# Reordered input projections, a smaller block solve, earlier feed-forward sums and a new load order in a hybrid decoder layer

## The chip, the cores and the metric

The kernel runs on one core of one Trainium2 chip. The metric is the device time of one execution in microseconds, on the core's own clock; the profile is of one execution of the same program.

## What is computed

One decoder layer on an input of 1024 tokens by 1024 features, float32. The reference, cut to what matters:

```python
h = rmsnorm(x, norm_mix)
proj = h @ w_in                                    # 1024 x 3360
q_nsa, kv_nsa, gate_nsa, qkv_gdn, z_gdn, b_gdn, a_gdn = split(proj)
o_nsa = rmsnorm(nsa_mixer(q_nsa, kv_nsa, gate_nsa, ...), nsa_norm)    # 8 heads of 64
o_gdn = gdn_mixer(qkv_gdn, z_gdn, b_gdn, a_gdn, ...)                  # 4 heads of 128
x = x + concat(o_nsa, o_gdn) @ w_out
u = causal_dwconv(rmsnorm(x, norm_ffn) @ ffn_up, ffn_conv)            # 2 x 2816 wide
gate, up = split(u)
x = x + (silu(gate) * up) @ ffn_down
return rmsnorm(x, norm_final)
```

nsa_mixer is sparse attention (compressed, selected and window branches). gdn_mixer is a gated delta rule: a causal convolution of width 4 on q, k and v, then for each chunk of 64 tokens a unit lower triangular system, solved by blocks of 32, and a state that is carried from chunk to chunk.

## The kernel before, in words

Tokens are worked on in 8 tiles of 128, or in two halves of 512. Large products run as float32r matmuls of 128 x 128 by 128 x 512. An operand is split into a high half (a cast to float32r on ScalarE, ACT) and a low half (the difference, on GpSimd, POOL, or on VectorE, DVE), and a product is the sum of high-high, high-low and low-high (`mm3`, from L122 to L128; the up product has the same in L1116, the down product in L1314). The program is given in the order of its functions; a planner with a model of the machine puts each engine's instructions in order, and `high_priority` and `issue_after` bias it. An engine then works through its own queue in order. All transfers are issued by SyncE (SP) from one queue.

**Input stage** (`phase_in`, L509). Activations are normalised and transposed into hH and hL. `proj_block` (L191) makes one block of 128 features by 512 tokens with 24 matmuls into one of two PSUM banks. `conv_block` (L448) loads and splits a tile of w_gdn (`split_weight`, L109; the POOL difference is L118), calls `proj_block`, copies the result twice to SBUF on ACT (L458, L463), applies three taps on DVE (L465), an activation (L468, L469), and stores to d_kqv. There are 12 tiles (0 to 3 make q, 4 to 7 k and 8 to 11 v), run for the first half of the tokens and then all for the second, each with its own load and split. The recurrence runs beside this with a higher priority: for a pair of tiles `gdn_pre` makes the blocks, `gdn_blocks` (L337) inverts 32 x 32 triangular blocks by 31 steps of two DVE instructions (L348, L350), with 32 columns spread over four partition groups and 8 columns a, and sends the result through DRAM (d_z) to `gdn_solve` (L355); `gdn_scan` carries the state. Further projections (z, q, compressed keys) fill the gaps.

**Attention** (`phase_attend`) holds the pools of its tiles, and pool og with the operand of the output product (mg). `phase_out` (L1006) does the output product of the last four tiles with operands mh and ml in a pool of its own (L1023, L1026), adds the residual, normalises (`norm_transpose`, L138) and puts high and low parts D (`put_parts`, L185).

**Feed-forward.** The up and down products use seven products instead of eight on 2 x 2 blocks, after two ordinary pairs of row tiles (`plain`) in the up product. The right-hand operands are sums of the four blocks B11, B12, B21 and B22 of the normalised input: T[0] to T[2], split in high and low parts. `norm_second` (L1049) makes them: s1 = B22 - B12 (L1088) as the transposes arrive, and the rest in `late` (L1092): 16 additions and subtractions with the split parts of D (`add`, L1073 to L1076) and three sets of four splits (L1070, L1071). `prepare` (L1183) makes the weight operands (L1140, L1142, L1153) of the next row tile, `convolve` and `put_away` do the convolution, the gate and the sums for the down product. `phase_down` (L1269) loads operands a_raw one pair at a time (L1301) and after each two entries of a queue of loads (L1294): weight quarters b11, b21, then the residual xr in eight row tiles, then b12 and b22. xr lies in the memory that the up product's row tiles held.

Of the kernel before, what the change touches and what calls it, by code (L numbers as in the profile page):

```python
# [46 lines left out]
def shape_constants():  # L47
# [11 lines left out]
    rho = i % 4  # L59
    for a in range(8):  # L60
        c[i, C_ZI + a * 32 + 8 * rho + a] = 1.0
# [129 lines left out]
def proj_block(K, w, b):  # L191

    wh, wl = w
    ps = K.pp.tile([P, 512], F32, name="proj_ps", tag="proj")
    d = slice(b * 512, (b + 1) * 512)
    mm3(K.nc, ps, [(wh[:, k * P:(k + 1) * P], wl[:, k * P:(k + 1) * P], K.hH[:, k, d], K.hL[:, k, d])
                   for k in range(NK)])
    return ps
# [138 lines left out]
def gdn_blocks(K, p):  # L337

    nc = K.nc
    db, dz = K.d_blk[p % 2], K.d_z[p % 2]  # L340
    bb = K.gt.tile([P, 32, 32], F32, name="bb", tag="bb")
    nc.sync.dma_start(bb, bc(db.rearrange("t b h j i -> (t b h) j i"), 1, 4))
    z = K.gt.tile([P, 8, 32], F32, name="zb", tag="zb")
    nc.vector.tensor_copy(z, K.zinit)
    for j in range(31):
        na, n = min(8, j + 1), 31 - j
        tmp = K.gt.tile([P, 8, 32], F32, name="ztmp", tag="ztmp", bufs=1)
        nc.vector.tensor_tensor(out=tmp[:, 0:na, 0:n], in0=bc(z[:, 0:na, j], 2, n), in1=bc(bb[:, j, j + 1:32], 1, na),  # L348
                                op=ALU.mult)
        nc.vector.tensor_tensor(out=z[:, 0:na, j + 1:32], in0=z[:, 0:na, j + 1:32], in1=tmp[:, 0:na, 0:n],  # L350
                                op=ALU.add)
    nc.sync.dma_start(dz.rearrange("t b h (r a) i -> (t b h r) (a i)", a=8), z.rearrange("p a i -> p (a i)"))


def gdn_solve(K, t, st):  # L355
# [3 lines left out]
    dz = K.d_z[t // 2 % 2][t % 2]  # L359
# [3 lines left out]
    for b in range(4):  # L363
        d = slice(32 * b, 32 * b + 32)
        nc.sync.dma_start(Z[d, :, d], dz[b].rearrange("h r i -> r h i"))
# [82 lines left out]
def conv_block(K, ct, b):  # L448
# [3 lines left out]
    ps = proj_block(K, split_weight(K, K.A["w_gdn"][ct]), b)  # L452
# [56 lines left out]
def phase_in(K, ctx):  # L509
# [45 lines left out]
    with ExitStack() as st:  # L555
# [17 lines left out]
        for ct in range(12):  # L573
            conv_block(K, ct, 0)
        for ct in range(12):
            conv_block(K, ct, 1)
# [386 lines left out]
def phase_attend(K, ctx):  # L963
    nc, tc = K.nc, K.tc
    mk = lambda n, b, **kw: ctx.enter_context(tc.tile_pool(name=n, bufs=b, **kw))
    for n in ("apl", "an", "aps", "asm", "ap", "og"):
        setattr(K, n, mk(n, 2 if n == "asm" else 1, side="right"))
# [38 lines left out]
def phase_out(K):  # L1006

    nc, tc, A = K.nc, K.tc, K.A
    with ExitStack() as st:
        xp = st.enter_context(tc.tile_pool(name="xo", bufs=2, side="right"))  # L1010
        po = st.enter_context(tc.tile_pool(name="po4", bufs=4, space=PSUM))
        px = st.enter_context(tc.tile_pool(name="pn2", bufs=4, space=PSUM))
        ws = K.ws
        for b, tiles in HALVES:
            for i in tiles:
# [5 lines left out]
                mh = xp.tile([P, 4, P], F32R, name="mh", tag="mh")  # L1021
                ml = xp.tile([P, 4, P], F32R, name="ml", tag="ml")
# [13 lines left out]
            if b:  # L1036
                norm_transpose(K, tiles, lambda j: K.x1[j],
                               lambda k, ps: put_parts(K, *K.D[k // 4][k % 4], ps,
                                                       K.vec[:, V_NFFN + k:V_NFFN + k + 1]), K.fw, px, "px", 4,
                               lambda j: row_tile(K, 4 + j))  # L1040


def row_tile(K, j):

    n = ("ga", "f_g", "f_u", "ga", "f_g", "f_u", "ga", "acc")[j]
    return K.fw.tile([P, 2 + SEQ], F32, name=n, tag=n, bufs={"ga": 3, "acc": 1}.get(n, 2))[:, 2:]


def norm_second(K):  # L1049
# [6 lines left out]
    K.T = [None] * 4  # L1056

    for j in (1, 2, 0, 3):
        h3 = K.late_pools.enter_context(tc.tile_pool(name=f"h3{j}", bufs=1))
        K.T[j] = [tuple(h3.tile([P, 512], F32R, name=f"t{n}{j}{k}") for n in "hl") for k in range(4)]  # L1060
# [12 lines left out]
    def add(out, x, j, k, op0, op1):  # L1073

        nc.vector.tensor_tensor(out=out, in0=x, in1=K.D[j][k][0].bitcast(F32), op=op0)
        nc.vector.tensor_tensor(out=out, in0=out, in1=K.D[j][k][1].bitcast(F32), op=op1)  # L1076

    def put(k, ps):
        g = K.vec[:, V_NFFN + k:V_NFFN + k + 1]
        if k < 4:  # L1080
            put_parts(K, *K.T[3][k], ps, g)
            b12[k] = scr("b12", 4)
            nc.scalar.activation(b12[k], ps, AF.Copy, scale=g)
            return
        k -= 4
        put_parts(K, *K.D[2][k], ps, g)
        s2 = s1[k] = scr("s1", 4)
        nc.vector.scalar_tensor_tensor(out=s2, in0=ps, scalar=g, in1=b12[k], op0=ALU.mult, op1=ALU.subtract)  # L1088
# [3 lines left out]
    def late():  # L1092
        for k in range(4):
            split(2, k, s1[k])
            add(b12[k], b12[k], 0, k, ALU.subtract, ALU.subtract)
            split(0, k, b12[k])
            add(s1[k], s1[k], 0, k, ALU.add, ALU.add)
            split(1, k, s1[k])
# [170 lines left out]
def phase_down(K, ctx, out):  # L1269
# [136 lines left out]
def open_common(K, ctx):  # L1406
# [36 lines left out]
    K.d_z = [dp.tile([2, 4, 4, 32, 32], F32, name=f"d_z{i}") for i in range(2)]  # L1443
# [3 lines left out]
def tile_hymba(ctx: ExitStack, tc: tile.TileContext, A, out):  # L1447
    K = Ctx()
    K.nc, K.tc, K.A = tc.nc, tc, A
    with ExitStack() as mix:  # L1450
        with ExitStack() as K.lctx:
# [6 lines left out]
            K.wn = mix.enter_context(tc.tile_pool(name="wn", bufs=2, side="right"))  # L1458
            with ExitStack() as st:
# [6 lines left out]
                for k in range(4)] for j in range(3)]  # L1466
        phase_out(K)
# [65 lines left out]
```

## Time and profile before

| | us |
|---|---|
| median of the runs (3) | 1486.92 |
| lowest and highest run | 1484.9, 1490.7 |
| the profiled execution | 1485.12 |
| its span, first to last instruction | 1483.3 |
| TensorE (PE) busy | 1423.7 (96%) |
| DVE, ACT, POOL busy | 1090.7, 688.1, 557.5 |

Times in the rows count from the start of the span. A group of instructions shows its line, engine, operation, out<-in, the shape and the count, then busy time, the mean of one in ns, and the idle time before it with what ended it. The matmuls of a group overlap: a mean of 400 ns in a dense stretch goes with one start every 0.23 us. The granted clock is the share of TensorE's full speed.

### The profile page before, as it was taken

To read this page: it belongs to the slowest core of one execution; us is meant where nothing else is said; L and a number is where in the kernel's file an instruction comes from. 1 tells how busy PE (TensorE), PEld (TensorE's weight loads), DVE (VectorE), ACT (ScalarE), POOL (GpSimd) and SP (SyncE) were. 2 spreads that over 40 slices of the span, in tenths; PEclk is the share of its full clock that TensorE was granted. 3 is DMA by queue.
4 is the path that set the end of the run, shared out by engine and by line. 5 is a ranking of instruction groups with operands and counts; after the bars stand their busy time and mean duration, and the time that the engine had idled before them with its cause. 6 is when DMAs were issued, how large, how long until landed. Compare 5 with 4: busy or idle time off the path is not lost.

```text
span 1483.3 us, 21381 instructions
## 1 busy us (share of the span) xinstructions
PE 1423.7 (96%) x7572; PEld 1144.8 (77%) x7572; DVE 1090.7 (74%) x2098; ACT 688.1 (46%) x1347; POOL 557.5 (38%) x547
## 2 busy tenths in 40 slices
PE   8998899999999999999999969999999999899997
PEld 8876677788877777777778848888888888778886
DVE  5768997887335686777546898888888887697656
ACT  7443343233233555678646444444444444333343
POOL 3356433344342343555555531111111112354444
PEclk9999999999999999999999989999999999999999
DMA  6245352344277544311225032322233326773334
GB/s 236 87 154 183 110 163 76 116 116 151 77 240 202 169 132 120 104 52 36 65 93 199 1 113 100 107 100 98 88 106 107 107 79 236 265 243 89 96 107 149
DMA packets 105627, 188.06 MB, mean 127 GB/s; under 512 B 17168, under 2 KB 52016, under 8 KB 105392
## 3 DMA queue, kind: packets, MB, share of 16 engines
q1 hardware_dynamic: 105520, 186.69, 38.9%
q8 instruction: 60, 0.98, 0.3%
q14 instruction: 47, 0.39, 0.1%
HBM read 135.00 MB, written 51.66 MB: 126 GB/s over the span
## 4 chain that ended last, share of the span: by engine, by line
PE 67%; DVE 16%; DMA 6%; issue 4%; ACT 4%; POOL 2%; SPq 0%; DVEq 0%; ACTq 0%; POOLq 0%
PE up_ps L1116 27%; PE dn_ps L1314 10%; PE po L890 4%; PE pt L877 4%; DVE cv_acc L465 3%; PE proj_ps L128 2%; PE proj_ps L126 2%; PE proj_ps L127 2%; PE s_ps L809 2%; PE s_ps L811 2%; DVE zb L350 1%; DVE ztmp L348 1%; PE og_ps L126 1%; PE og_ps L127 1%; PE og_ps L128 1%
## 5 line engine op out<-in xcount | busy, mean ns | idle before, releaser
L1314 PE MATMUL dn_ps<-d_op 128*128 128x512 f32 x924 | 213.9, 393 | 4.5 <-ACT d_op L1305 1.9
L1314 PEld LDWEIGHTS dn_ps<-d_op 128*128 128x128 f32 x924 | 174.8, 190 | 43.1 <-DVE d_op L1308 2.6
L128 PE MATMUL proj_ps<-hH,w_l 128*128 128x512 f32 x384 | 157.2, 409 | 6.9 <-POOL w_l L118 6.9
L126 PE MATMUL proj_ps<-hH,w_h 128*128 128x512 f32 x384 | 155.5, 407 | 3.6 <-ACT cv_acc L463 3.3
L127 PE MATMUL proj_ps<-hL,w_h 128*128 128x512 f32 x384 | 154.9, 403 | 0.0
L1306 POOL TENSOR_TENSOR d_op<-a_raw,d_op 128x1024 fp32r<-128x1024 f32 (+1 forms) x42 | 105.1, 2504 | 124.0 <-ACT d_op L1305 104.8
L1116 PE MATMUL up_ps<-th,op_h 128*128 128x512 f32 x336 | 133.3, 398 | 11.8 <-ACT op_h L1140 11.8
L1116 PE MATMUL up_ps<-tl,op_h 128*128 128x512 f32 x336 | 133.3, 397 | 0.0
L1116 PE MATMUL up_ps<-th,op_l 128*128 128x512 f32 x336 | 132.7, 396 | 0.0
L118 POOL TENSOR_TENSOR w_l<-w_raw,w_h 128x1024 fp32r<-128x1024 f32 (+2 forms) x46 | 109.5, 2386 | 53.5 <-ACT w_h L116 51.9
L1308 DVE TENSOR_TENSOR d_op<-b,d_op 128x1024 fp32r<-128x1024 f32 (+1 forms) x42 | 81.9, 1954 | 49.2 <-ACT d_op L1307 43.3
L1116 PE MATMUL up_ps<-dh,op_h 128*128 128x512 f32 x288 | 113.0, 398 | 1.4 <-ACT op_h L1140 1.4
L1116 PE MATMUL up_ps<-dl,op_h 128*128 128x512 f32 x288 | 113.7, 396 | 0.0
L1116 PE MATMUL up_ps<-dh,op_l 128*128 128x512 f32 x288 | 110.4, 395 | 0.0
L1228 DVE SCALAR_TENSOR_TENSOR ga<-f_g,vec,ga 128x1024 f32<-128x1024 f32 x44 | 91.0, 2068 | 11.1 <-ACT ga L1226 10.4
L1161 POOL MEMSET f_u<- 128x2 f32 x22 | 2.2, 100 | 253.0 <-DVE acc L1228 160.3
L128 PEld LDWEIGHTS proj_ps<-hH,w_l 128*128 128x128 f32 x384 | 74.1, 193 | 27.0 <-POOL w_l L118 10.9
L1140 ACT ACTIVATE op_h<-w_raw 128x1024 fp32r<-128x1024 f32 (+1 forms) x64 | 58.8, 923 | 71.8 <-PE up_ps L1116 69.9
L465 DVE SCALAR_TENSOR_TENSOR cv_acc<-cv_raw,vec,cv_acc 128x512 f32<-128x512 f32 x72 | 76.6, 1063 | 18.4 <-ACT cv_acc L463 17.6
L126 PEld LDWEIGHTS proj_ps<-hH,w_h 128*128 128x128 f32 x384 | 74.0, 193 | 19.4 <-ACT cv_acc L463 4.7
L1305 ACT ACTIVATE d_op<-a_raw 128x1024 fp32r<-128x1024 f32 (+1 forms) x42 | 41.3, 985 | 101.7 <-PE dn_ps L1314 47.8
L127 PEld LDWEIGHTS proj_ps<-hL,w_h 128*128 128x128 f32 x384 | 74.2, 193 | 15.6 <-DVE hL L188 0.4
(334 smaller groups left out, 3474.2 us busy)
## 6 DMA issues: line engine op xcount, KB each, us to landing
w_raw<-in_w_up_dram SPq DMA_DIRECT2D x44, 512.0 KB, 3.3
a_raw<-d_a SPq DMA_DIRECT2D x35, 512.0 KB, 3.6
w_raw<-in_w_gdn_dram SPq DMA_DIRECT2D x24, 512.0 KB, 3.7
d_a<-ga SPq DMA_DIRECT2D x44, 256.0 KB, 2.0
b<-in_w_down_dram SPq DMA_DIRECT2D x20, 512.0 KB, 6.6
d_a<-so SPq DMA_DIRECT2D x33, 256.0 KB, 2.0
qT<-d_q SPq DMA_DIRECT2D x32, 256.0 KB, 5.6
mg<-d_mix SPq DMA_DIRECT2D x16, 512.0 KB, 3.9
```

Source lines behind the costliest of these rows:

```text
L118: (low or nc.gpsimd).tensor_tensor(out=wl, in0=raw, in1=wh.bitcast(F32), op=ALU.subtract)
L126: nc.tensor.matmul(out, ah, bh, start=(i == 0), stop=False)
L127: nc.tensor.matmul(out, ah, bl, start=False, stop=False)
L128: nc.tensor.matmul(out, al, bh, start=False, stop=(i == n - 1))
L465: nc.vector.scalar_tensor_tensor(out=acc, in0=raw[:, j:j + 512], scalar=tap(j), in1=acc, op0=ALU.mult, op1=ALU.add)
L877: nc.tensor.transpose(pt[0:kk, h, :], src[h], K.ident)
L890: last = nc.tensor.matmul(po[64 * par:64 * par + 64], v, pT[:, par::2], start=(last is None or first), stop=(left == 0))
L1116: mm = lambda a, b, start, stop: nc.tensor.matmul(out, a, b, start=start, stop=stop, skip_group_check=not first)
L1228: nc.vector.scalar_tensor_tensor(out=a, in0=raw[:, j:j + SEQ], scalar=tap(j), in1=a, op0=ALU.mult, op1=ALU.add)
L1306: nc.gpsimd.tensor_tensor(out=al, in0=raw, in1=ah.bitcast(F32), op=ALU.subtract)
L1308: nc.vector.tensor_tensor(out=bl, in0=b[js.start], in1=bh.bitcast(F32), op=ALU.subtract)
L1314: one = lambda a, b, start, stop: nc.tensor.matmul(ps, a, b, start=start, stop=stop, skip_group_check=not first)
```

## The change

It has these parts. The title that it came with names grouped value products too; no line of the diff touches the value products of the attention.

- `proj_block`: the products with the low half of the weight come last.
- `phase_in`, `conv_block`: tiles 0 to 7 for the first half, then 8 to 11 for both halves with one load and split, then 0 to 7 for the second half.
- `gdn_blocks`, `gdn_solve`: column 4a + r in partition group r, so that step j needs j // 4 + 1 columns; d_z is laid out by row; bb is loaded in four pieces.
- `phase_attend`, `phase_out`: pool og outlives the attention and holds mh and ml; the PSUM pools of `phase_out` wait tile by tile.
- `phase_out`, `norm_second`: a copy b11 of block B11; t0 = B12 - B11, s1 = B22 - B12 and b12 = B22 - t0 are formed from PSUM; `late` only splits.
- `phase_down`: the residual is loaded in eight pieces of two row tiles by 512 columns, two of them after b11 and six at the end of the queue.

```diff
-    rho = i % 4
+    rho = i // 32
     for a in range(8):
-        c[i, C_ZI + a * 32 + 8 * rho + a] = 1.0
+        c[i, C_ZI + a * 32 + 4 * a + rho] = 1.0
...
-    mm3(K.nc, ps, [(wh[:, k * P:(k + 1) * P], wl[:, k * P:(k + 1) * P], K.hH[:, k, d], K.hL[:, k, d])
-                   for k in range(NK)])
+    jobs = [(wh, h, k) for k in range(NK) for h in (K.hH, K.hL)] + [(wl, K.hH, k) for k in range(NK)]
+    for n, (w, h, k) in enumerate(jobs):
+        K.nc.tensor.matmul(ps, w[:, k * P:(k + 1) * P], h[:, k, d], start=(n == 0), stop=(n == len(jobs) - 1))
...
-    nc.sync.dma_start(bb, bc(db.rearrange("t b h j i -> (t b h) j i"), 1, 4))
+    for r in range(4):
+        nc.sync.dma_start(bb[32 * r:32 * r + 32], db.rearrange("t b h j i -> (t b h) j i"))
...
-        na, n = min(8, j + 1), 31 - j
+        na, n = j // 4 + 1, 31 - j
...
-    nc.sync.dma_start(dz.rearrange("t b h (r a) i -> (t b h r) (a i)", a=8), z.rearrange("p a i -> p (a i)"))
+    nc.sync.dma_start(dz.rearrange("(a r) t b h i -> (r t b h) a i", r=4), z)
...
-        nc.sync.dma_start(Z[d, :, d], dz[b].rearrange("h r i -> r h i"))
+        nc.sync.dma_start(Z[d, :, d], dz[:, b])
...
-        for ct in range(12):
-            conv_block(K, ct, 0)
-        for ct in range(12):
-            conv_block(K, ct, 1)
+        for cts, bs in ((range(8), (0,)), (range(8, 12), (0, 1)), (range(8), (1,))):
+            for ct in cts:
+                w = split_weight(K, A["w_gdn"][ct], low=None)
+                for b in bs:
+                    conv_block(K, ct, b, w)
...
-        po = st.enter_context(tc.tile_pool(name="po4", bufs=4, space=PSUM))
-        px = st.enter_context(tc.tile_pool(name="pn2", bufs=4, space=PSUM))
+        po = st.enter_context(tc.tile_pool(name="po4", bufs=4, space=PSUM, reuse_waits="tile"))
+        px = st.enter_context(tc.tile_pool(name="pn2", bufs=4, space=PSUM, reuse_waits="tile"))
...
-                mh = xp.tile([P, 4, P], F32R, name="mh", tag="mh")
-                ml = xp.tile([P, 4, P], F32R, name="ml", tag="ml")
+                mg = K.og.tile([P, 4, 2 * P], F32R, name="mg", tag="mg", bufs=2)
+                mh, ml = mg[:, :, 0:P], mg[:, :, P:2 * P]
...
+                    put_parts(K, *K.D[k // 4][k % 4], ps, g)
+                    if k < 4:
+                        nc.scalar.activation(K.b11[k], ps, AF.Copy, scale=g)
...
+def sum_tile(K, j, k, part, dtype=F32R):
+    return K.h3[j].tile([P, 512], dtype, name=f"t{part}{j}{k}", tag=f"{part}{k}")
...
+    t0 = [sum_tile(K, 2, k, "h", F32) for k in range(4)]
+    K.T[3] = parts(3)
...
+        diff = lambda out, x: nc.vector.scalar_tensor_tensor(out=out, in0=ps, scalar=g, in1=x, op0=ALU.mult, op1=ALU.subtract)
         if k < 4:
             put_parts(K, *K.T[3][k], ps, g)
             b12[k] = scr("b12", 4)
             nc.scalar.activation(b12[k], ps, AF.Copy, scale=g)
+            diff(t0[k], K.b11[k])
             return
         k -= 4
         put_parts(K, *K.D[2][k], ps, g)
-        s2 = s1[k] = scr("s1", 4)
-        nc.vector.scalar_tensor_tensor(out=s2, in0=ps, scalar=g, in1=b12[k], op0=ALU.mult, op1=ALU.subtract)
+        s1[k] = scr("s1", 4)
+        diff(s1[k], b12[k])
+        diff(b12[k], t0[k])
...
     def late():
-        for k in range(4):
-            split(2, k, s1[k])
-            add(b12[k], b12[k], 0, k, ALU.subtract, ALU.subtract)
-            split(0, k, b12[k])
-            add(s1[k], s1[k], 0, k, ALU.add, ALU.add)
-            split(1, k, s1[k])
+        for j, src in ((1, b12), (0, t0), (2, s1)):
+            K.T[j] = parts(j)
+            for k in range(4):
+                split(j, k, src[k])
         st.close()
...
-    queue = [(t[js.start], src) for t, js, src in b[0] + b[1]] + [(xr[:, i], K.d_x1[i]) for i in range(NT)]
+    res = lambda r, c: [(xr[:, i:i + 2, 512 * c:512 * c + 512],
+                         K.d_x1[i:i + 2, :, 512 * c:512 * c + 512].rearrange("i p c -> p i c"))
+                        for i in (4 * r, 4 * r + 2)]
+    queue = [(t[js.start], src) for t, js, src in b[0] + b[1]]
+    queue[6:6] = res(0, 0)
     queue += [(t[js.start], src) for p in zip(b[2], b[3]) for t, js, src in p]
+    queue += res(1, 0) + res(1, 1) + res(0, 1)
...
-    K.d_z = [dp.tile([2, 4, 4, 32, 32], F32, name=f"d_z{i}") for i in range(2)]
+    K.d_z = [dp.tile([32, 2, 4, 4, 32], F32, name=f"d_z{i}") for i in range(2)]
...
+        K.T = [None] * 4
+        K.h3 = {1: mk("h31")}
+
+        K.b11 = [sum_tile(K, 1, k, "l", F32) for k in range(4)]
```

## Rows read from the trace of the kernel before

**Rows 1.** The page: busy time by engine, share of the span, instructions.

```profile
PE 1423.7 (96%) x7572; PEld 1144.8 (77%) x7572; DVE 1090.7 (74%) x2098; ACT 688.1 (46%) x1347; POOL 557.5 (38%) x547
```

**Rows 2.** Busy time by stretches: us, PE, PEld, DVE, ACT, POOL (instructions), clock, DMA share, GB/s.

```profile
100.00:240.00 140.00, 127.24 (x652) 97.67 (x650) 126.08 (x297) 55.62 (x112) 61.89 (x53) 0.95 0.46 146
240.00:460.00 220.00, 210.69 (x1358) 175.09 (x1358) 126.09 (x326) 68.09 (x192) 88.71 (x78) 0.98 0.47 139
...
854.00:872.00 18.00, 4.83 (x11) 3.31 (x11) 18.00 (x18) 8.92 (x12) 11.79 (x9) 0.63 0.23 86
872.00:1251.00 379.00, 379.00 (x1625) 304.89 (x1624) 318.24 (x329) 176.02 (x215) 62.16 (x58) 1.00 0.31 107
1251.00:1330.00 79.00, 74.49 (x314) 59.86 (x312) 60.05 (x38) 29.26 (x32) 33.87 (x13) 0.96 0.77 278
```

**Rows 3.** Waits of PE, 100 to 240 us: us in total, times, longest.

```profile
PE proj_ps L128 <- POOL w_l L118: 6.6, 8, 2.0
PE proj_ps L126 <- ACT cv_acc L463: 3.3, 3, 1.5
```

**Rows 4.** Waits of PE, 774 to 900 us.

```profile
PE up_ps L1116 <- ACT op_h L1140: 13.2, 2, 11.8
PE out_ps L126 <- ACT mh L1023: 0.9, 1, 0.9
```

**Rows 5.** DVE and POOL in order of time in the convolutions: start, us, instruction.

```profile
141.10 2.39 POOL L118 TENSOR_TENSOR w_l<-w_raw,w_h 128x1024 fp32r<-128x1024 f32 x1 [1.97 <-ACT w_h L116]
141.14 2.48 DVE L348 TENSOR_TENSOR ztmp<-zb,bb 128x112 f32<-128x112 f32 x1
143.65 0.27 DVE L350 TENSOR_TENSOR zb<-zb,ztmp 128x112 f32<-128x112 f32 x1
...
148.20 0.35 DVE L348 TENSOR_TENSOR ztmp<-zb,bb 128x192 f32<-128x192 f32 x1
```

**Rows 6.** Groups of DVE's instructions, 100 to 240 us.

```profile
L465 DVE SCALAR_TENSOR_TENSOR cv_acc<-cv_raw,vec,cv_acc 128x512 f32<-128x512 f32 x49 | 50.6, 1034 | 6.4 <-ACT cv_acc L463 6.0
L348 DVE TENSOR_TENSOR ztmp<-zb,bb 128x112 f32<-128x112 f32 (+29 forms) x62 | 26.7, 430 | 1.0
```

**Rows 7.** DMA issues of the whole span: count, KB each, median us to landing.

```profile
d_z<-zb SPq DMA_DIRECT2D x4, 128.0 KB, 3.4
Zx<-d_z SPq DMA_DIRECT2D x32, 16.0 KB, 1.8
```

**Rows 8.** ACT, SP and PE in order of time, late part of the kernel.

```profile
813.68 0.70 ACT L1083 ACTIVATE b<-nt_ps,vec 128x512 f32<-128x512 f32 x1
...
852.91 0.80 SPq L1134 DMA_DIRECT2D w_raw<-in_w_up_dram  x2
...
1279.46 3.14 SPq L1294 DMA_DIRECT2D x<-d_x  x6
...
1294.71 1.42 PE L1314 MATMUL dn_ps<-d_op 128*128 128x512 f32 x4 [1.86 <-ACT d_op L1305]
```

**Rows 9.** Groups of DVE's instructions, 820 to 846 us.

```profile
L1075 DVE TENSOR_TENSOR s<-s,dh 128x512 f32<-128x512 f32 x4 | 4.9, 1232 | 0.0
L1076 DVE TENSOR_TENSOR b<-b,dl 128x512 f32<-128x512 f32 x4 | 4.9, 1229 | 0.0
L1075 DVE TENSOR_TENSOR b<-b,dh 128x512 f32<-128x512 f32 x4 | 4.7, 1166 | 0.0
L1076 DVE TENSOR_TENSOR s<-s,dl 128x512 f32<-128x512 f32 x4 | 3.7, 954 | 0.0
L188 DVE SCALAR_TENSOR_TENSOR dl<-nt_ps,vec,dh 128x512 fp32r<-128x512 f32 x4 | 3.0, 743 | 5.5 <-ACT dh L187 5.5
```

**Rows 10.** SP's own waits, 800 to 860 us.

```profile
SPq L1134 <- DVE tl L1071: 40.1, 1, 40.1
```

**Rows 11.** The chain that ended last, 1270 to 1300 us: start, us, what.

```profile
1286.24 11.05 DMA a_raw<-d_a
```

More of the change, by code (lines that the diff above doesn't have):

```diff
@@ L358, in gdn_solve @@
     B, wq, keg, vv = st.B, st.wq, st.keg, st.vv
-    dz = K.d_z[t // 2 % 2][t % 2]
+    dz = K.d_z[t // 2 % 2][:, t % 2]
     Z, zt, qs = K.Zx[t % 2], K.zt, K.qs
@@ L445, in gdn_out, with conv_block @@
     nc.sync.dma_start(K.d_mix[t], st.wq)
-def conv_block(K, ct, b):
+def conv_block(K, ct, b, w):
     nc = K.nc
     which, h = ct // 4, ct % 4
-    ps = proj_block(K, split_weight(K, K.A["w_gdn"][ct]), b)
+    ps = proj_block(K, w, b)
     raw = K.scr.tile([P, 3 + 512], F32, name="cv_raw", tag="cv_raw")
@@ L965, in phase_attend @@
     mk = lambda n, b, **kw: ctx.enter_context(tc.tile_pool(name=n, bufs=b, **kw))
-    for n in ("apl", "an", "aps", "asm", "ap", "og"):
+    for n in ("apl", "an", "aps", "asm", "ap"):
         setattr(K, n, mk(n, 2 if n == "asm" else 1, side="right"))
@@ L1036, in phase_out, with put @@
             if b:
[L1037 to L1040, printed above, removed]
+                def put(k, ps):
+                    g = K.vec[:, V_NFFN + k:V_NFFN + k + 1]
+                    put_parts(K, *K.D[k // 4][k % 4], ps, g)
+                    if k < 4:
+                        nc.scalar.activation(K.b11[k], ps, AF.Copy, scale=g)
+                norm_transpose(K, tiles, lambda j: K.x1[j], put, K.fw, px, "px", 4, lambda j: row_tile(K, 4 + j))
 def row_tile(K, j):
@@ L1046, in row_tile @@
     return K.fw.tile([P, 2 + SEQ], F32, name=n, tag=n, bufs={"ga": 3, "acc": 1}.get(n, 2))[:, 2:]
+def sum_tile(K, j, k, part, dtype=F32R):
+    return K.h3[j].tile([P, 512], dtype, name=f"t{part}{j}{k}", tag=f"{part}{k}")
 def norm_second(K):
     nc, tc = K.nc, K.tc
[L1056 to L1060, printed above, removed]
+    for j in (2, 0, 3):
+        K.h3[j] = K.late_pools.enter_context(tc.tile_pool(name=f"h3{j}", bufs=1))
+    parts = lambda j: [(sum_tile(K, j, k, "h"), sum_tile(K, j, k, "l")) for k in range(4)]
+    t0 = [sum_tile(K, 2, k, "h", F32) for k in range(4)]
+    K.T[3] = parts(3)
     K.us = K.late_pools.enter_context(tc.tile_pool(name="us", bufs=4, side="right"))
@@ L1071, in split @@
         (nc.vector if j == 1 else nc.gpsimd).tensor_tensor(out=l, in0=src, in1=h.bitcast(F32), op=ALU.subtract)
-    def add(out, x, j, k, op0, op1):
-        nc.vector.tensor_tensor(out=out, in0=x, in1=K.D[j][k][0].bitcast(F32), op=op0)
-        nc.vector.tensor_tensor(out=out, in0=out, in1=K.D[j][k][1].bitcast(F32), op=op1)
     def put(k, ps):
         g = K.vec[:, V_NFFN + k:V_NFFN + k + 1]
+        diff = lambda out, x: nc.vector.scalar_tensor_tensor(out=out, in0=ps, scalar=g, in1=x, op0=ALU.mult, op1=ALU.subtract)
         if k < 4:
@@ L1458, in tile_hymba @@
             K.wn = mix.enter_context(tc.tile_pool(name="wn", bufs=2, side="right"))
+            K.og = mix.enter_context(tc.tile_pool(name="og", bufs=1, side="right"))
             with ExitStack() as st:
```

## The prediction, made before the changed kernel was run

> **What bounds the kernel now.** I read the page first. TensorE (PE) is busy for 1423.7 of the span's 1483.3 us [rows 1], so at most 59.6 us are to be had, plus what matmuls lose at a low clock. The edits remove no matmul, so they can only close gaps, and the next view, the busy time by stretches, says where these are [rows 2]. In the up product (872 to 1251 us) PE never rests: 1625 matmuls in 379 us, 0.233 us each; nothing is to be had there. Four stretches have gaps: the convolutions (100 to 240: 12.8 us idle, granted clock 0.95), the recurrence (240 to 460: 9.3 us, 0.98), the entry of the up product (854 to 872: 11 matmuls in 18 us, where 77 would fit at 0.233; 15.4 us lost, clock 0.63 of full speed, a mix of the levels 2.4 and 1.2 GHz), and the entry of the down product (1251 to 1330: 4.5 us idle, clock 0.96; its 314 matmuls would take 73.2 us at 0.233, so 5.8 are lost). Third, the waits of PE: in 100 to 240 the longest is for the low halves of weights, which POOL makes (6.6 us), then 3.3 us for ACT, which empties PSUM behind VectorE's (DVE's) taps [rows 3]; in the up entry it is 13.2 us for the operands' high halves [rows 4].
>
> The second engine in the convolutions is DVE: 126.1 of 140 us [rows 2]. Part of that isn't work. A step on 112 elements takes 0.27 us and one on 192 takes 0.35, but the 112-element step at 141.14 takes 2.48: it starts just behind POOL's weight subtraction (141.10, 2.39 us) and ends with it [rows 5]. The taps (128 x 512) average 1034 ns in this stretch [rows 6].
>
> **The change part by part.**
>
> *Input stage.* (1) In every projection the 8 products with the low weights go last, behind 16 others, 16 x 0.233 = 3.7 us of cover. The longest wait for a low half is 2.0 us [rows 3], so the 6.6 us should go; next late is the PSUM bank (3.3 us). (2) Weight tiles 8 to 11 are loaded and split once for both halves of the tokens: 4 loads of 24, 4 ACT casts and 4 POOL subtractions fewer. Each subtraction holds DVE for up to 2.48 - 0.27 = 2.2 us [rows 5]; I take 1.8 (not each meets a DVE step at its start), 7.2 us of DVE. (3) The block solves keep their 62 steps per pair of tiles, but step j works on j//4 + 1 columns instead of min(8, j + 1): summed over j, 1560 elements against 3156, in two instructions. The slope is (0.35 - 0.27) / 80 = 1.0 ns per element [rows 5], so 2 x 1596 x 1.0 = 3.2 us per pair; the 62 products of two pairs, and as many sums, lie before 240 us [rows 6]: 6.4 us of DVE there and 6.4 later, where DVE is busy only 126 of 220 us [rows 2] and hides it.
>
> So 13.6 us leave a DVE that is busy for nine tenths of the stretch, and the waits for POOL have cover. PE's loss there is 12.8 us idle and some 3 at the low clock. I take 9 before 240 us and 2 after; bounds 0 (PE waits as long for the next thing) and 27 (all gaps of both stretches, 22.1, and 5 of clock, half of what it lacks: 0.05 x 140 + 0.02 x 220 = 11).
>
> Costs. The z store now writes runs of 128 bytes where it wrote 1 KB: 1024 runs instead of 128. Before, it lands in 3.4 us; the loads of z, 16 KB in 128 runs of 128 bytes, in 1.8 [rows 7]. So the new one costs between 3.4 us (same bytes) and 8 x 1.8 = 14.4 us (runs one after another). I take 4.4, near the row with the same bytes and direction. Of four stores only the first has little else in flight: 1 us. The load of bb in four pieces adds three issues on SP per pair, some 0.4 us each by SP's rows [rows 8], 1.2 us in a queue with free time; hidden by the taps, 4.8 us if bare. The halves of q and k for late tokens come four blocks later and v earlier; the cover is the solves. Sum of the stage: 9 + 2 - 1 = 10 us gained.
>
> The Trainium skill, "DMA: Bandwidth & Descriptors", section "Specifications", says that a transfer under 512 bytes falls below line rate, since the engine reads, modifies and writes. It speaks against the z store; no row here shows it apart from the fixed time. By it the store would lie toward the upper end, which is a rival below; by the rows it is 1 us.
>
> *Behind the attention.* Casts of the last four tiles go into a buffer that outlives the attention's pools, and the PSUM pools are released tile by tile: the only wait of PE that these touch is 0.9 us [rows 4]. I take 1; bounds 0 and 1.
>
> *Sums of the up product.* The late part had 16 additions on DVE, all with both inputs in SBUF: 4.9 + 4.9 + 4.7 + 3.7 = 18.2 us [rows 9]. They are replaced by 8 differences that read PSUM and one tile, as the low halves (dl) there do: 0.74 us each [rows 9], 5.9 us. Four of these (t0) fit into the 5.5 us in which DVE waits for ACT [rows 9], so DVE's queue shortens by 18.2 - 3.0 = 15.2 us, or by 16 x 0.74 - 3.0 = 8.8 if POOL's holds only move to other steps. The wait behind this: SP's loads of weight tile 2 are issued at 852.91 [rows 8], after SP has waited 40.1 us for the last low half that DVE makes [rows 10], since they go into memory that the sums occupied; only then can ACT cast the halves that PE waits for. With 15.2 us less ahead of it that half is ready at 838; POOL's eight splits are as many as before, so I say 840, early enough for a PE that needs the operands at 854. What is late next is DVE, with convolution and operand sums of two tiles behind each other. Price: 4 copies to b11 on ACT at 0.70 us [rows 8], 2.8 us between the transposes and the first operand casts; PE has output products to run meanwhile; up to 2.8 if that cover is short. I take 12 of the 15.4; bounds 0 and 15.4.
>
> *Down product.* SP now asks for the residual in eight pieces: two after the first weight quarter, six last; before, all eight stood ahead of the second column half. Their memory comes free only at 1279, so six of the eight (3 MB) start in one burst and the others behind [rows 8], and the operand asked for at 1286.24 lands after 11.05 us [rows 11]; PE has a gap at 1294.7 [rows 8]. Afterwards two of the eight stand there, and six weight loads, some of which can go before 1279. The queue is as long by count, so I take only 2 of the 5.8 us; bounds +6 and -11 (one more operand behind the two early pieces, at that row's price).
>
> **Sum.** 10 + 1 + 12 + 2 = 25 us. The profiled execution took 1485.1 us, 1.8 around its span and 1.8 less than the median of the runs, so 1485.1 - 25 = 1460.1 by its own time and 1462 by the median.
>
> **The rivals.**
> - *The input stage gives nothing* (the recurrence or the PSUM banks are what PE waits for): 1462 + 10 = 1472. For it: 3.3 us of waits for ACT stay [rows 3]. Against: DVE at nine tenths. 0.13.
> - *The up entry's gap stays* (the loads wait for another buffer, or the halves for POOL): 1462 + 12 = 1474. For it: POOL's splits are as many. 0.09.
> - *Slower: recurrence starved.* Tiles 4 to 7 need the last q and k, which now come four blocks later; a block takes 24 x 0.233 = 5.6 us of PE alone, and up to 8 with the recurrence between. If the 32 us stand bare in 200 to 460, the stage loses 32 and its gain: 1462 + 10 + 32 = 1504. It decides once more than 25 + 7.4 us are bare. Against: the work of tiles 0 to 3 stands in between, and PE idles only 9.3 us in 240 to 460 [rows 2]. 0.05.
> - *The short runs.* All four z stores at the upper bound: 4 x 11 = 44 us of the recurrence's chain; half bare gives 1462 + 22 = 1484, all bare 1506. This is the way in which the Trainium skill's rule on short transfers ("DMA: Bandwidth & Descriptors", "Specifications") would decide. 0.05.
> - *No effect*: gaps close and open elsewhere, since the order of each engine's queue is planned anew (and the value products of the title are not in the diff): 1487. 0.06.
>
> **Numbers.** The forecast has 0.62 and its own range is 1450 to 1471. The range 1444 to 1482 takes in the first two rivals and most of the bounds upward; left out are about 0.07 below (all upper bounds at once give 1487 - 49 = 1438) and 0.12 above. A difference under 0.5%, 7.4 us, can't be told from none here. Faster by more than that: 0.62 + 0.13 + 0.09 less tails, 0.82. Within: 0.06 and half of the short runs and tails, 0.10. Slower: 0.08.
>
> **What would show it.** Right: DVE busy some 14 us less before 240 us; PE's wait for low weights under 1 us; 20 weight loads for the convolutions; SP's loads of weight tile 2 near 840 and no wait of PE over 3 us at the up entry, with the clock at 1.0 there; z stores landing within 6 us. Wrong: a new PE wait over 5 us in 200 to 460 on the scan or on a DMA; an operand load over 11 us at the down entry; the up stretch of 379 us longer, which would mean DVE's backlog follows PE into it.

## The result, and the profile after

The changed kernel takes 1464.2 us (median of four runs, 1461.0 to 1469.1) where the kernel before, beside it, takes 1487.7: a ratio of 0.9845, 95% interval 0.981 to 0.988. The profiled execution has a span of 1459.7 us against 1483.3. The forecast was 1462.

Where the 23.6 us of the two spans came from is read off TensorE's (PE's) order of time, by the first and last matmul of each stage:

| | before | after | gained | forecast |
|---|---|---|---|---|
| start to the first score of the attention | 455.3 | 442.0 | 13.3 | 10 |
| from there to the first up product (attention, out product) | 344.8 | 345.9 | -1.1 | 1 |
| first to last up product | 460.1 | 450.3 | 9.8 | 12 |
| last up to last down product | 214.1 | 212.1 | 2.0 | 2 |
| tail | 9.0 | 9.4 | -0.4 | 0 |

The page's first part after, beside [rows 1]:

```profile
PE 1411.6 (97%) x7572; PEld 1139.8 (78%) x7572; DVE 1063.1 (73%) x2090; ACT 687.7 (47%) x1347; POOL 548.1 (38%) x543
```

The matmuls are as many, yet PE is busy 12.1 us less: half of the gain in this pair of executions is not idle time, but fewer matmuls at the low clock (granted over the span: 0.99 of full speed, 0.98 before). That share is the less certain one, since executions of one kernel differ in it: the changed kernel's four ran at 0.985 to 0.990. The stretches after that answer to [rows 2] (columns as there; they lie earlier by about what was gained till then):

```profile
100.00:240.00 140.00, 129.14 (x725) 101.76 (x724) 120.36 (x317) 51.24 (x107) 57.34 (x51) 0.98 0.44 133
...
840.00:858.00 18.00, 13.29 (x48) 9.39 (x47) 18.00 (x18) 8.03 (x11) 9.16 (x6) 0.91 0.25 74
858.00:1239.00 381.00, 381.00 (x1642) 308.95 (x1641) 317.13 (x329) 176.23 (x215) 60.26 (x57) 1.00 0.32 114
1239.00:1317.00 78.00, 73.07 (x317) 58.83 (x316) 62.88 (x37) 29.93 (x32) 38.54 (x15) 1.00 0.70 243
```

The convolutions run 725 matmuls in 140 us instead of 652, the up entry 48 instead of 11 in 18 us. VectorE (DVE) is still busy for 120.4 of the 140 us, and for all of the 18. Next, PE's three largest waits from 40 to 456 us ("issue" is time in which it waited for nothing that the profile shows), and the group of products with the low weights, whose last number is PE's idle time just before them:

```profile
PE tr_ps L256 <- issue: 3.7, 3, 1.9
PE kk_ps L287 <- issue: 2.5, 1, 2.5
PE tr_ps L256 <- DVE vv L333: 1.7, 1, 1.7
```
```profile
L199 PE MATMUL proj_ps<-hH,w_l 128*128 128x512 f32 x384 | 102.5, 400 | 0.0
```

The wait for POOL's low halves [rows 3] is gone; the small waits left belong to the recurrence. But the hold of [rows 5] is not gone (POOL, then DVE, in order of time):

```profile
145.41 2.38 POOL L118 TENSOR_TENSOR w_l<-w_raw,w_h 128x1024 fp32r<-128x1024 f32 x1 [1.44 <-ACT w_h L116]
```
```profile
145.56 2.33 DVE L351 TENSOR_TENSOR ztmp<-zb,bb 128x72 f32<-128x72 f32 x1
147.92 0.23 DVE L353 TENSOR_TENSOR zb<-zb,ztmp 128x72 f32<-128x72 f32 x1
```

A step on 72 elements takes 2.33 us behind POOL's subtraction, and the next one 0.23. The DMA issues, as in [rows 7]:

```profile
w_raw<-in_w_gdn_dram SPq DMA_DIRECT2D x20, 512.0 KB, 3.9
...
d_z<-zb SPq DMA_DIRECT2D x4, 128.0 KB, 3.9
Zx<-d_z SPq DMA_DIRECT2D x32, 16.0 KB, 1.8
```

The up entry: SP's wait, its loads of weight tile 2, and PE's waits from 780 to 880 us, beside [rows 10], [rows 8] and [rows 4].

```profile
SPq L1144 <- DVE tl L1085: 22.1, 1, 22.1
```
```profile
823.70 0.81 SPq L1144 DMA_DIRECT2D w_raw<-in_w_up_dram  x2
```
```profile
PE up_ps L1126 <- ACT op_h L1150: 2.2, 1, 2.2
PE up_ps L1126 <- DVE f_g L1163: 1.0, 1, 1.0
PE up_ps L1126 <- POOL op_l L1152: 0.9, 1, 0.9
PE up_ps L1126 <- DVE op_l L1152: 0.7, 1, 0.7
```

The loads start 35.8 us behind the first up product (787.90) instead of 52.8 (852.91 behind 800.14), and the waits of 13.2 us in all (11.8 in one piece) have become four short ones of 4.8, of which two name DVE.

### The profile page after: what moved, and what is told of

The parts are those of the page before. It is cut to its first block, busy times and chain, and to the rows that moved or that the text cites. A ratio compares the mean times of both kernels' runs of the same rounds, so it can differ in the third digit from the quotient of the medians.

```text
span 1459.7 us, 21369 instructions
## 1 busy us (share of the span) xinstructions
PE 1411.6 (97%) x7572; PEld 1139.8 (78%) x7572; DVE 1063.1 (73%) x2090; ACT 687.7 (47%) x1347; POOL 548.1 (38%) x543
## 4 chain that ended last, share of the span: by engine, by line
PE 73%; DVE 14%; DMA 5%; issue 3%; ACT 2%; POOL 2%; SPq 1%; DVEq 0%; POOLq 0%; ACTq 0%
PE up_ps L1126 27%; PE proj_ps L199 11%; PE dn_ps L1329 10%; PE po L895 4%; PE pt L882 4%; DVE cv_acc L468 2%; PE s_ps L814 2%; PE s_ps L816 2%; DMA b<-in_w_down_dram 1%; DVE b L1336 1%; PE s_ps L418 1%; DVE zb L353 1%; DVE ztmp L351 1%; PE m_ps L411 1%; PE cmp_ps L687 1%
## 5 line engine op out<-in xcount | busy, mean ns | idle before, releaser
L118 POOL TENSOR_TENSOR w_l<-w_raw,w_h 128x1024 fp32r<-128x1024 f32 (+2 forms) x42 | 99.9, 2384 | 44.3 <-ACT w_h L116 22.8
L199 PE MATMUL proj_ps<-hH,w_l 128*128 128x512 f32 x384 | 102.5, 400 | 0.0
L1238 DVE SCALAR_TENSOR_TENSOR ga<-f_g,vec,ga 128x1024 f32<-128x1024 f32 x44 | 89.5, 2035 | 12.1 <-ACT ga L1236 11.4
L199 PEld LDWEIGHTS proj_ps<-hL,w_h 128*128 128x128 f32 x384 | 72.7, 190 | 15.2 <-DVE hL L188 0.5
L199 PEld LDWEIGHTS proj_ps<-hH,w_l 128*128 128x128 f32 x384 | 70.9, 189 | 14.8 <-issue 0.7
L887 ACT ACTIVATE pT<-pt 128x512 f32<-128x512 f32 x104 | 59.4, 589 | 44.9 <-PE pt L882 44.3
```

The source lines that it names most:

```text
L118: (low or nc.gpsimd).tensor_tensor(out=wl, in0=raw, in1=wh.bitcast(F32), op=ALU.subtract)
L199: K.nc.tensor.matmul(ps, w[:, k * P:(k + 1) * P], h[:, k, d], start=(n == 0), stop=(n == len(jobs) - 1))
L887: nc.scalar.activation(pT[0:kk], pt[0:kk], AF.Copy)
L1238: nc.vector.scalar_tensor_tensor(out=a, in0=raw[:, j:j + SEQ], scalar=tap(j), in1=a, op0=ALU.mult, op1=ALU.add)
```

## The experiments

Theory: in the input stage DVE's time is what lacks, and part of that time is DVE held by POOL subtractions; at the up entry it is the same engine's queue. The rival in each case: the removed wait only makes room for the next. Every ratio is taken against the kernel before on the same chip (medians of 1486.9 to 1488.8 us). "Lows" are the low halves of operands. The last four columns are read off one profiled execution of each kernel; "attention at" is its first score product, the other three are the stages of the table above.

| kernel | us | ratio, 95% interval | attention at | to first up | up product | down |
|---|---|---|---|---|---|---|
| changed | 1464.2 | 0.9845, 0.981-0.988 | 442.0 | 345.9 | 450.3 | 212.1 |
| old order of products | 1472.8 | 0.9908, 0.989-0.993 | 449.2 | 345.5 | 453.1 | 211.9 |
| two passes | 1467.5 | 0.9867, 0.984-0.990 | 444.0 | 348.1 | 450.5 | 213.3 |
| old solve | 1467.2 | 0.9865, 0.984-0.990 | 448.1 | 350.0 | 452.1 | 212.0 |
| old sums | 1472.2 | 0.9902, 0.989-0.992 | 441.0 | 349.2 | 459.5 | 211.8 |
| old load order | 1465.3 | 0.9855, 0.984-0.987 | 439.4 | 348.3 | 450.4 | 213.9 |
| old pools | 1466.6 | 0.9873, 0.985-0.990 | 440.1 | 350.1 | 452.0 | 212.5 |
| before, lows on DVE | 1474.8 | 0.9905, 0.988-0.993 | 436.4 | 349.1 | 460.0 | 214.4 |
| lows on DVE | 1452.9 | 0.9777, 0.975-0.981 | 429.7 | 344.9 | 451.8 | 212.4 |
| and idle POOL reads | 1481.6 | 0.9959, 0.994-0.998 | 456.7 | 348.7 | 451.0 | 212.7 |
| and idle POOL memsets | 1456.3 | 0.9781, 0.975-0.981 | 431.1 | 349.4 | 450.7 | 213.5 |
| lows and sums on DVE | 1444.6 | 0.9718, 0.970-0.974 | 431.2 | 344.3 | 444.1 | 212.5 |
| nearly all lows on DVE | 1430.1 | 0.9609, 0.958-0.963 | 431.3 | 338.2 | 443.9 | 205.9 |

The column "to first up" scatters from 344.3 to 350.1 over kernels whose code there is the same, or the same but for the pools and the copies b11; a difference of a few us in it tells nothing. The profiled executions also lie off their medians: 1473.5 us for the old solve (median 1467.2), 1470.6 for before with lows on DVE (1474.8), 1461.6 for the changed kernel (1464.2). So "attention at" holds a few us of scatter too, most of it in PE's busy time, which goes with the granted clock.

**Old order of products** in a projection:

```diff
-    jobs = [(wh, h, k) for k in range(NK) for h in (K.hH, K.hL)] + [(wl, K.hH, k) for k in range(NK)]
...
+    mm3(K.nc, ps, [(wh[:, k * P:(k + 1) * P], wl[:, k * P:(k + 1) * P], K.hH[:, k, d], K.hL[:, k, d])
+                   for k in range(NK)])
```

> The changed kernel with the 24 products of a projection in the old order (high, high-low, low for each slice), all else as changed. By the forecast's term (1) PE again waits for the low halves that POOL makes, 6.6 us in 100 to 240 us, and the attention begins some 6 us later (448 instead of 442): about 1470 us. Rival: VectorE sets the pace of the convolutions, and the wait for the low half only takes the place of waits for PSUM and for ACT: the wait shows (4 to 7 us) but the attention begins within 1.5 us of 442, and the time stays at 1463 to 1466.

The kernel is 8.6 us slower, clear of the noise, and the attention begins 7.2 us later: the size that the forecast gave, but not by its wait. PE's waits from 40 to 456 us, and PE, PEld, DVE, ACT, POOL from 40 us to the attention:

```profile
PE tr_ps L254 <- DVE at L299: 3.6, 2, 2.1
PE cmp_ps L685 <- DMA w_raw<-in_w_dram: 3.5, 1, 3.5
PE q_ps L373 <- DVE zt L371: 2.7, 1, 2.7
...
PE proj_ps L128 <- POOL w_l L118: 0.2, 1, 0.2
```
```profile
40.00:449.16 409.16, 388.99 (x2297) 320.07 (x2295) 272.06 (x695) 142.02 (x344) 165.78 (x152) 0.97 0.44 134
```

The wait for the low half is 0.2 us. The loss is 4.8 us more idle time (409.16 - 388.99 = 20.2 against 15.4) in waits of the recurrence and on a DMA, and 2.4 us more busy time of as many matmuls. Neither theory foresaw that, and DVE, at 272.1 us, is not busier than in the changed kernel (275.3). The orders of DVE, ACT and POOL differ between the two kernels too; which of those differences costs the 7 us stays open.

**Two passes, and the old solve:**

```diff
-        for cts, bs in ((range(8), (0,)), (range(8, 12), (0, 1)), (range(8), (1,))):
...
+        for b in range(2):
+            for ct in range(12):
+                conv_block(K, ct, b, split_weight(K, A["w_gdn"][ct], low=None))
```


> The changed kernel with the convolutions in two passes of twelve blocks again (24 loads and splits instead of 20), all else as changed. By the forecast's term (2) four more POOL subtractions hold VectorE for 1.8 us each, 7.2 us: VectorE is busy for 7 us more before 460 us and the attention begins 3 to 7 us later, 1467 to 1471. Rival: the late q and k of the new order cost the recurrence what the fewer splits give; then the old order is no slower, 1461 to 1466.

```diff
-        na, n = j // 4 + 1, 31 - j
+        na, n = min(8, j + 1), 31 - j
...
-    K.d_z = [dp.tile([32, 2, 4, 4, 32], F32, name=f"d_z{i}") for i in range(2)]
+    K.d_z = [dp.tile([2, 4, 4, 32, 32], F32, name=f"d_z{i}") for i in range(2)]
```


> The changed kernel with the block solve as it was (min(8, j + 1) columns per step, z stored in runs of 1 KB, bb in one load). By the forecast's terms: 3.2 us more of VectorE per pair of tiles, 12.8 in all, of which 6.4 before 240 us count, and 1 us back for the z store: attention 3 to 6 us later, 1467 to 1470. Rival: the solves lie where VectorE has room and the 128-byte runs of the z store cost the recurrence its gain: 1462 to 1465, z stores back at 3.4 us.

The same row for before, the changed kernel, two passes and the old solve, each from 40 us to its attention, so that each holds the same work:

```profile
40.00:455.30 415.30, 392.94 (x2293) 319.48 (x2291) 292.94 (x693) 148.29 (x351) 177.02 (x157) 0.97 0.44 136
```
```profile
40.00:441.96 401.96, 386.61 (x2294) 317.24 (x2293) 275.28 (x690) 144.81 (x344) 166.51 (x152) 0.98 0.44 135
```
```profile
40.00:443.99 403.99, 384.88 (x2295) 316.57 (x2294) 280.59 (x690) 148.17 (x348) 177.82 (x156) 0.99 0.46 139
```
```profile
40.00:448.11 408.11, 391.44 (x2292) 322.42 (x2291) 288.26 (x689) 144.06 (x344) 167.86 (x152) 0.97 0.44 133
```

The third number is DVE. Two passes cost it 5.3 us (forecast 7.2), the old solve 13.0 (forecast 4 x 3.2 = 12.8). The attention begins 2.0 and 6.1 us later; of the 6.1, 4.8 are PE's busy time at a clock of 0.97 against 0.98 (391.4 against 386.6) and 1.3 idle time. By the times (+3.3 and +3.0 us) neither is told from the changed kernel: the intervals overlap. So DVE's work is shown in its size, and what it is worth in time is not. For the rivals, that the late q and k or the short runs eat the gain, these runs show nothing.

**Old sums, old load order, old pools:**

One line of each of the three edits, in this order:

```diff
+    def add(out, x, j, k, op0, op1):
...
-    queue[6:6] = res(0, 0)
...
-        po = st.enter_context(tc.tile_pool(name="po4", bufs=4, space=PSUM, reuse_waits="tile"))
+        po = st.enter_context(tc.tile_pool(name="po4", bufs=4, space=PSUM))
```

> The changed kernel with the sums of the operand tiles in the old form (16 additions from both halves, no b11, buffers allotted as before), all else as changed. By the forecast's term the up entry loses 12 us again: no change before the out product ends, loads of weight tile 2 some 12 us later after the first up product than now, a wait of PE for operand halves of 8 to 13 us, the up product 9 to 12 us longer, 1473 to 1477. Rival: a part of the gain at the up entry came with the casts' longer-lived buffer and the pools released by tile, not with the sums: the up product only 3 to 6 us longer, 1467 to 1470.

> The changed kernel with the down product's load order as it was (all eight residual tiles ahead of the second column half). By the forecast 2 us are lost again after the up product, 1465 to 1467, with six residual loads in one burst. Rival: the residual's place in the queue decides more than that, 1469 to 1473; second rival: VectorE's sums set the pace of the down entry and the order is worth nothing, 1462 to 1465.

> The changed kernel with the casts of the last four tiles and the PSUM pools of the out product as they were, all else as changed. By the forecast 1 us at the handover from attention to the out product: 1464 to 1466. Rival: nothing, since the wait there was not removed by the change (1.25 us on VectorE now, 0.9 us on ScalarE before): 1462 to 1465, the same gap between the last attention product and the first out product. A time above 1468 would mean that the pools, not the sums, opened the up entry.

With the old sums the up product is 9.2 us longer, and the waits of the kernel before return to the digit (SP's, then PE's):

```profile
SPq L1144 <- DVE tl L1081: 40.1, 1, 40.1
```
```profile
PE up_ps L1126 <- ACT op_h L1150: 13.2, 2, 11.8
```

So the gain there is the sums' and not the pools'. (The edit also allots the sums' buffers as before, so the shorter queue of DVE and the new places are undone together.) The old load order costs 1.8 us between the last up and the last down product, as forecast, too little for the times to show. The column "down" bears it out: the three kernels with the old order (the kernel before is one) have 213.9 to 214.4 there, the ten with the new one 211.8 to 213.5 (without the last row, whose down product was changed). The entry itself, changed and with the old order, in the same window:

```profile
1228.50:1307.50 79.00, 74.07 (x321) 59.47 (x320) 64.37 (x42) 29.96 (x33) 33.81 (x14) 1.00 0.81 285
```
```profile
1228.50:1307.50 79.00, 72.10 (x314) 58.20 (x312) 59.84 (x37) 29.00 (x31) 33.35 (x13) 1.00 0.78 281
```

PE is idle for 4.9 us with the new order and for 6.9 with the old. The old pools change nothing at the handover: the gap from the last attention product to the first out product is 0.9 us there, 1.3 in the changed kernel and 0.9 before. Its 2.4 us are within the scatter.

**Lows on DVE.** The 20 subtractions of the convolutions' weights move from POOL:

```diff
-                w = split_weight(K, A["w_gdn"][ct], low=None)
+                w = split_weight(K, A["w_gdn"][ct], low=nc.vector)
```

> The changed kernel with the low halves of the 20 convolution weights subtracted on VectorE instead of POOL. A test of the 1.8 us by which a POOL subtraction is said to hold VectorE: a 128 x 1024 subtraction with both inputs in SBUF takes VectorE 1.1 to 1.3 us by itself. If the hold is 1.8 us or more, VectorE's other steps shorten (taps from 1.0 us towards 0.8) by more than the subtractions add, busy time before 240 us falls by up to 10 us and the time by 2 to 8: 1456 to 1462. If the hold is under 1.2 us on average, VectorE is busier and the time is 1464 to 1472.

The attention begins 12.3 us earlier and the kernel is 11.3 us faster, more than expected. From 40 us on (the stretch, DVE's taps and its new subtractions; first the taps of the changed kernel up to its attention):

```profile
L468 DVE SCALAR_TENSOR_TENSOR cv_acc<-cv_raw,vec,cv_acc 128x512 f32<-128x512 f32 x72 | 68.0, 944 | 12.0 <-ACT cv_acc L466 11.0
```
```profile
40.00:429.67 389.67, 382.25 (x2295) 316.36 (x2294) 265.75 (x707) 145.22 (x344) 125.09 (x134) 0.99 0.46 139
```
```profile
L468 DVE SCALAR_TENSOR_TENSOR cv_acc<-cv_raw,vec,cv_acc 128x512 f32<-128x512 f32 x72 | 58.1, 807 | 2.7 <-ACT cv_acc L466 1.7
...
L118 DVE TENSOR_TENSOR w_l<-w_raw,w_h 128x1024 fp32r<-128x1024 f32 x18 | 23.9, 1327 | 5.0 <-PE proj_ps L199 4.7 <-ACT w_h L116 0.3
```

DVE got 18 instructions of 23.9 us in this stretch and is busy 9.5 us less. So its other steps had lost 23.9 + 9.5 = 33.4 us, 1.86 us for each subtraction on POOL; a subtraction on DVE costs 1.33. The trace of the changed kernel shows the loss step by step: 20 of its 72 taps overlap a POOL step with two inputs and take 1453 ns on average, the 42 that overlap no POOL step 748. DVE steps with one input in PSUM don't show it: vn<-vv,m_ps takes 683 ns beside such a POOL step and 682 without.

**The same edit alone, on the kernel before:**

> The kernel before with one edit: the low halves of the 24 convolution weights on VectorE. If VectorE's held time is what the input stage lacked, this alone gives most of what the three input edits gave and the attention begins at 441 to 446 instead of 455: 1472 to 1478. Rival: with the low product third of each slice PE now waits for VectorE's queue, and the larger block solve keeps VectorE full: the attention begins after 450, 1482 or more.

1474.8 us, 13.9 less than the kernel before, and in the profiled execution the attention begins 18.9 us earlier (436.4):

```profile
40.00:436.36 396.36, 381.73 (x2297) 314.52 (x2296) 285.56 (x717) 147.63 (x348) 130.39 (x134) 1.00 0.47 143
```

Of the 18.9, 7.7 us are idle time of PE (22.4 to 14.6) and 11.2 are busy time, at a clock of 1.00 against 0.97; the three input edits took 7.0 of idle time. So this one edit gave about what they gave. It is not DVE's held time alone: the edit also ends PE's wait for POOL's low halves, 6.9 us from 40 to 456 us before, and the run does not tell the two apart.

**Idle work on POOL,** added behind each split of "lows on DVE": four subtractions that read two inputs, as shown, or in their place eight memsets of the same tile.

```diff
+    for c in range(0, n, 256) if extra else ():
+        dum = pool.tile([P, 256], BF16, name="dum", tag="dum", bufs=1)
+        nc.gpsimd.tensor_tensor(out=dum, in0=raw[:, c:c + 256], in1=wh[:, c:c + 256].bitcast(F32), op=ALU.subtract)
```

> The kernel with the convolutions' low halves on VectorE, with idle work put back on POOL: behind each of the 20 splits four subtractions of 128 x 256 with two inputs in SBUF, whose result nobody reads. By the theory that such POOL steps hold VectorE, VectorE's own steps between 100 and 240 us get longer (taps from 0.82 to 0.87 us or more on average, single steps of 1.2 to 2.5 us again), the attention begins 6 to 14 us later than with the halves on VectorE alone and the time goes to 1458 to 1468. Rival: what the halves on VectorE saved was the wait for POOL itself (its queue and its 2.4 us per subtraction), not VectorE's time; then idle work that nobody waits for costs nothing: 1450 to 1456.

> The same with eight POOL memsets of 128 x 256 behind each split in place of the subtractions: POOL is as occupied in instructions, but reads nothing from SBUF. By the theory of a hold between readers of SBUF the time stays within 3 us of the kernel with the halves on VectorE alone, 1450 to 1456, and the taps at 0.80 to 0.84 us. Rival: anything on POOL holds VectorE, or POOL's queue delays other steps; then 1458 or more.

With reads (stretch, DVE's taps, POOL's idle work):

```profile
40.00:456.65 416.65, 390.96 (x2320) 322.08 (x2319) 296.53 (x717) 145.36 (x346) 197.18 (x206) 0.98 0.43 130
```
```profile
L471 DVE SCALAR_TENSOR_TENSOR cv_acc<-cv_raw,vec,cv_acc 128x512 f32<-128x512 f32 x72 | 63.8, 886 | 1.5 <-ACT cv_acc L469 0.4 <-issue 0.2
```
```profile
L121 POOL TENSOR_TENSOR dum<-w_raw,w_h 128x256 bf16<-128x256 f32 x72 | 75.5, 1048 | 25.5 <-issue 12.4 <-ACT w_h L116 8.9 <-POOL cv_raw L463 0.7
```

With memsets (the last two lines are the idle work over the whole span, memsets and then reads: count, ns at least, in the middle and at most, first and last start):

```profile
40.00:431.08 391.08, 383.69 (x2312) 318.00 (x2311) 268.63 (x718) 145.99 (x345) 152.19 (x225) 1.00 0.46 138
```
```profile
L121 POOL MEMSET dum<- 128x256 bf16 x91 | 28.5, 313 | 4.6
```
```profile
L121 POOL MEMSET dum<- x160: 306/312/740, 1.8 to 77.2; 128x256 bf16 x160
```
```profile
L121 POOL TENSOR_TENSOR dum<-w_raw,w_h x80: 722/1053/1833, 18.3 to 202.2; 128x256 bf16<-128x256 f32 x80
```

With reads whose result nobody uses, DVE is busy 30.8 us longer up to the attention (296.5 against 265.75, some 6 of it in ten more instructions that fall into the stretch), and the kernel takes 28.7 us more (27.3 with each taken against the kernel before on its own chip). So the loss is not a wait for POOL's result.

The memsets are a weaker test than they were meant to be. They depend on nothing, and the planner put all of them before 77.5 us, so in most of the convolutions none ran; that the time is not told from "lows on DVE" (1456.3 and 1452.9, intervals alike) shows little. What they did meet can still be read: 12 taps overlap a memset and take 750 ns, against 746 for the 46 that overlap nothing on POOL; in the run with reads, 32 taps overlap an idle subtraction and take 984 against 742.

The Trainium skill, "SBUF — State Buffer", section "Who interferes with whom", says that a DVE instruction with two SBUF inputs contends with a GpSimd instruction that reads SBUF, not with one that only writes it. The taps, which have two inputs in SBUF, agree: 984 ns beside reads and 750 beside memsets.

**Sums, then nearly all low halves, on DVE:** in the sums both subtractions of the code (12 splits, 4 second terms); then the default engine of the weight splits and the down product's operands too (the up operands that POOL makes stay there).

```diff
-        (nc.vector if j == 1 else nc.gpsimd).tensor_tensor(out=l, in0=src, in1=h.bitcast(F32), op=ALU.subtract)
+        nc.vector.tensor_tensor(out=l, in0=src, in1=h.bitcast(F32), op=ALU.subtract)
...
-        nc.gpsimd.tensor_tensor(out=al, in0=raw, in1=ah.bitcast(F32), op=ALU.subtract)
+        nc.vector.tensor_tensor(out=al, in0=raw, in1=ah.bitcast(F32), op=ALU.subtract)
```

> The kernel with the convolutions' low halves on VectorE, and in addition all the sums' low halves and the sum's second term on VectorE instead of POOL (12 splits and 4 differences of 128 x 512). By the theory that a POOL step with two inputs in SBUF holds VectorE for longer than VectorE would need for it (0.7 us by the rows of such steps), VectorE is through its backlog at the up entry earlier: the waits of PE for operand halves there (4.8 us in all) fall below 3 and the time falls by 1 to 4 us against the kernel with the convolutions' halves alone. Rival: the up entry's backlog has more steps now and grows by up to 8 us: 1 to 5 us slower than that kernel.

> The fastest version so far (low halves of the convolutions and all steps of the sums on VectorE) with the low halves of all other weights and of the down product's operands on VectorE too. If a POOL subtraction always costs VectorE more than the step costs it itself, the gaps of PE at the down entry (4.3 us waiting for low halves) shrink and the time falls to 1437 to 1443. Rival: in the attention and in the first half of the down product VectorE is the busier engine and has no room for the added steps: 1446 to 1453.

The first shortens the up product by 7.7 us (expected 1 to 4): PE's waits at the up entry fall to 0.5 us. In the second the rest of the way shortens by 6.1 us before the up product, within reach of that column's scatter, and by 6.6 in the down product. The low halves of the down product's operands that DVE makes (128 x 1024, in the first with a smaller form among them), in the first from 1215 to 1300 us, in the second over the whole span:

```profile
L1323 DVE TENSOR_TENSOR d_op<-b,d_op 128x1024 fp32r<-128x1024 f32 (+1 forms) x15 | 30.0, 2013 | 13.9 <-ACT d_op L1322 9.6 <-issue 4.3
```
```profile
L1321 DVE TENSOR_TENSOR d_op<-a_raw,d_op 128x1024 fp32r<-128x1024 f32 x35 | 42.8, 1223 | 49.9 <-ACT d_op L1320 49.9
L1323 DVE TENSOR_TENSOR d_op<-b,d_op 128x1024 fp32r<-128x1024 f32 x35 | 42.6, 1218 | 0.1
```

Beside POOL one subtraction took DVE 2.01 us; now two take 2.44, and no wait of PE is left at the down entry. This version, 1430.1 us, is 34 us faster than the changed kernel and 58.6 faster than the one before on its chip.

## Why the prediction was right

The time, the direction and the size of three of the four stages came out, though not each by the step given. The sum is closer than its terms, whose misses (3.3 us more, then 2.1 and 2.2 less) partly cancel; that much is luck. And half of the gain is busy time at a better clock, where the forecast spoke above all of gaps.

- **Input stage, 10 forecast, 13.3 measured.** By the 625th product of the projections, at 236 us before, PE was 8.0 us ahead, where 9 were forecast till 240; behind that came 5.3 more, where 2 were forecast less 1. DVE's work fell by 17.7 us (292.9 to 275.3) where the steps give 7.2 + 12.8 = 20. The size of step (3) held, 13.0 for 12.8. The 1.8 us per POOL subtraction lies in the range of what the runs give: 1.86 by the lows on DVE, 5.3 / 4 = 1.3 by the two passes. **Step (1) was right in size and wrong in its reason:** the wait is gone, but does not return with the old order (0.2 us for 6.6), and yet 7.2 us do; that the sizes meet is luck as far as these runs show. The sign given, DVE 14 us less before 240 us, was badly put: DVE is busy only 5.7 us less there (126.1 to 120.4), since later work moves in. Work has to be compared, not stretches. Of the gain, 7.0 us are idle time (22.4 to 15.4) and 6.3 are busy time at a better clock (392.9 to 386.6; 0.97 to 0.98), of which the forecast had counted little.
- **z store.** A median of 3.9 us, near the 4.4 taken, far from the upper bound of 14.4; one of the four took 6.3, just over the 6 given as a sign. What the short runs cost is not pinned down: 0.5 us against the kernel before (3.4), 2.2 against the old solve (1.7); over all kernels here the medians are 2.3 to 3.9 with short runs and 1.7 to 3.4 with long ones. The rival by the Trainium skill's rule on short transfers ("DMA: Bandwidth & Descriptors", "Specifications") did not decide. The trace agrees with its direction at most, by these medians.
- **Behind the attention, 1 forecast, none found.** The gap did not shrink (0.9 to 1.3 us); PE now waits for DVE at og instead of ACT at mh.
- **Sums, 12 forecast, 9.8 measured** (9.2 by the undoing). The 15.2 us out of DVE's queue fit: the loads came 17.0 us earlier against the first up product. What was mis-sized is what is late next: the sign "no wait over 3 us" holds, but the four waits add up to 4.8 us and the sign on the clock failed, 0.91 in 840 to 858 and not 1.0. The forecast named that DVE backlog; when the sums' steps left POOL too, 7.7 us more went.
- **Down product, 2 forecast, 2.0 measured,** 1.8 by the undoing. Against the kernel before, PE's idle time at the entry did not fall (4.5 us in 79 [rows 2], 4.9 in 78); what fell is busy time, at a clock of 1.00 against 0.96. With the old order undone alone, it is the idle time that differs (6.9 and 4.9). One sign given for being wrong did show: the operand asked for at 1261.46 us landed after 12.3, where over 11 was the mark. None of PE's waits there names that load.
- **Rivals.** The starved recurrence did not show: no wait of PE over 3.7 us in all from 40 to 456. The up gap went with the sums. Short runs: see the z store.

## What to carry to other kernels

When a DVE step takes several times what its shape takes elsewhere and ends with a POOL instruction, count that time as DVE's cost of the POOL instruction; work given to POOL to relieve DVE can cost DVE as much as doing it itself or more (1.3 to 1.86 us against 1.33 here). Test it with idle work on POOL, once with reads and once without, and look in the trace where the idle work ran: work that depends on nothing may be put ahead of the stage that it was to disturb. When an edit plans all orders anew, undo one part at a time and compare equal work, since the wait that an edit removes by name may not be what it is worth.

## Unexpected

That three edits to the input stage were worth no more than moving one instruction form to another engine: 7.0 us of PE's idle time against 7.7 on the kernel before. And that idle reads on POOL cost nearly one to one, 30.8 us of DVE and 28.7 us of the kernel's time, though DVE was idle for 120 of the 417 us up to the attention there: the steps that became longer lay on the path that sets the stage's time.
